# Two feed-forward blocks with mixers: the second mixer's norms by row sums on all partitions, its substitution loop in three runs

## The chip, the core and the metric

One core of a Trainium2 chip runs the whole program in one launch. The metric is device time in microseconds of that core; smaller is better. All names of engines are those of the profile: PE multiplies matrices (PEld is its weight load), DVE is VectorE, ACT is ScalarE, POOL is GpSimd, SP issues most DMAs.

## The reference, cut to what matters

A sequence of 512 tokens of width 1024 goes through two blocks, each: half a SwiGLU feed-forward, a mixer, half a SwiGLU feed-forward, a norm. All is float32. The change lies in the mixer of the second block, in two norms of it:

```
def short_conv_mixer(b_gate, c_gate, h, conv_w, out_gain):       # width 512, 8 groups of 64
    y = b_gate * causal_depthwise_conv(c_gate * h, conv_w)
    return rmsnorm per group of 64 channels of y, times out_gain
def gated_deltanet_mixer(q, k, v, z, b, a, ...):                 # 4 heads of 128
    q, k, v = split(silu(causal_depthwise_conv(qkv)));  q, k = l2norm(q), l2norm(k)
    o = gated_delta_rule_chunked(q, k, v, g, beta)   # per chunk: solve (I + lower) x = rhs, then a scan
    return rmsnorm(o, norm_w) * silu(z)              # over the 128 channels of a head
h = h + concat(y_conv, y_gdn) @ w_mix_out
```

Each rmsnorm is y * (mean(y*y) + eps) ** -0.5 * gain. The triangular solve is done by substitution inside blocks of 16 rows, then by merging blocks in three levels.

## The kernel before, in words

Activations lie with channels on the 128 partitions and the 512 tokens along the row, so a norm over channels needs a sum across partitions. That sum is made on PE. Every projection is made in three products of 128x512 in the type fp32r (high times high, high times low, low times high parts); a product of two float32 operands is issued by PE as two products, so one statement in the code shows as two instructions in the trace. A transpose of float32 shows as one.

`mix2` (L640) is the second mixer. PE's order in it is written by hand: `main` (L1023) runs 28 projections of 24 products each (`gproj`, L799, products at L806), and after every product `tick` (L1029) lets at most one waiting step of another generator run. A step that returns a lag n is due n ticks later. So 672 ticks make the stage, and the table `LAG` (L34) places every other product between the projections' ones. The generators are `chain` (L817, one for each of the 4 heads, at most 3 alive), `decays` (L726), and `short_end` (L970, one for each of the 4 short convolutions). The other engines' order is not by hand: the framework's scheduler sets it in advance, earlier statements first where they are ready.

The steps of a head's chain that the texts below speak of: the head's decays (L776 to L786: a spread of columns, Exp on ACT, four DVE operations at L783) and k's transposes (L823); q times k (L835); the sums of k's squares (`tok_sums`, L842); k times k and `u_` (L851, L854); transposes of v (L859) and of `u_` (L886); the products that give `bx` (L892); the substitution loop on DVE (L897 to L902: 15 turns of a product and a sum); three merging levels (L912, L914, ACT copies at L919 and L920, L924); `wt` (L929, L931); the scan over 4 chunks, each a product into `pv` (L940, L942), a copy `vn` by ACT (L943), after r0 ticks the products L949 and L954 and the state's update on DVE (L951, L953), which the next chunk's L942 reads after r1 ticks.

The head's norm at L957 to L966: squares, after o0 ticks `tok_sums` (L695, one product of 128x128 by 128x1 for each of 4 token blocks, `tok`=1 tick apart, so that a projection's product lies between), then `rsqrt_cols` (L237: a reciprocal root by 11 small DVE operations after one for scale and eps), after o1 ticks `spread2` (L704: four transposes at L267 that bring the columns back to all partitions), and one DVE operation with the gain. `short_end` does the same with two groups of 64: the spread is then eight float32 products (L270).

`rms_rows` (L281) is the form that the kernel uses elsewhere, for the norms ahead of the projections: the squares are split in a high and a low part (one ACT, one DVE operation), two products with a 128x128 matrix of minus ones (`onesr`, L278) give the sums on all partitions at once, then Ln, Exp and Square on ACT (L287 to L289) and two DVE operations (L290, L291) make the reciprocal root with one Newton step. Products into PSUM in `mix2` use three banks of the tag "g".

Of the kernel before, what the change touches and what calls it, by code (L numbers as in the profile page):

```python
# [10 lines left out]
F32 = mybir.dt.float32  # L11
F32R = mybir.dt.float32r
I32 = mybir.dt.int32
AF = mybir.ActivationFunctionType
ALU = mybir.AluOpType

P = 128
T = 512
NT = T // P
# [4 lines left out]
EPS = 1e-6  # L24
# [6 lines left out]
LIVE = 3  # L31
NWARM = 9
SCRATCH = 1024
LAG = dict(d0=4, d1=30, d2=81, d3=7, d4=10, tok=1, c0=7, c1=3, c2=3, c3=2, c5=17, c6=26, c7=46, c8=11, c9=9, c10=11, r0=3, r1=4, o0=9, o1=27, s0=14, s1=22)  # L34
MIXORD = (4, 5, 6, 0, 1, 2, 3, 7)
WINDOWS = (2, 4, 8, 16)
MAGIC = float(0x5F3759DF)
# [87 lines left out]
class Kern:  # L125
# [4 lines left out]
    def nm(self, s):  # L130
        self.n += 1
        return f"{s}_{self.n}"
# [8 lines left out]
def tile_blocks(ctx: ExitStack, tc: tile.TileContext, ins, out, stop=None):  # L141
    nc = tc.nc
    K = Kern(ctx, tc)
    nm = K.nm
    SM = [("sm", 1)]

    const = K.pool(ctx, "const", far=True)
# [4 lines left out]
    tp = K.pool(ctx, "tmp", far=True)  # L152
# [7 lines left out]
    def vcol(name, i=0, n=1):  # L160
        o = VEC_COLS[name][0] + i
        return vec[:, o : o + n]
# [3 lines left out]
        return cst[:, o : o + w]  # L166

    h = [hp.tile([P, T], F32, name=f"h{k}") for k in range(KD)]
    idle = const.tile([P, P], F32, name="idle")
    nc.vector.memset(idle, 0.0)  # L170
    nc.vector.memset(ones1, 1.0)
    warm = const.tile([P, 1], F32, name="warm")
# [2 lines left out]
    ident = cst_("ident")  # L175
# [61 lines left out]
    def rsqrt_cols(src, n, scale, eps=EPS):  # L237

        v = rp.tile([P, n], F32, name=nm("rv"), tag="rv", bufs=4)
        nc.vector.tensor_scalar(v, src, scale, eps, ALU.mult, ALU.add)  # L240
        return newton(v, n)
# [12 lines left out]
            yf = b  # L254
        return b

    def spread(psp, cols, groups=1):

        ps = psp.tile([P, T], F32, name=nm("pb"), tag=SM[0][0], bufs=SM[0][1])
        spread_into(ps, cols, groups)  # L260
        return ps

    def spread_into(ps, cols, groups=1):
        m = P // groups
        for t in range(NT):
            if groups == 1:
                nc.tensor.transpose(ps[:, t * P : (t + 1) * P], cols[:, t, :].to_broadcast([P, P]), ident)  # L267
                continue
            for g in range(groups):
                nc.tensor.matmul(ps[g * m : (g + 1) * m, t * P : (t + 1) * P],  # L270
                                 cols[:, t, g : g + 1].to_broadcast([P, m]), ident, start=True, stop=True)

    def row_sums(psp, parts, of, tag=None):

        tag, bufs = tag or SM[0]
        ps = psp.tile([P, T], F32, name=nm("pr"), tag=tag, bufs=bufs)
        for j, part in enumerate(parts):
            nc.tensor.matmul(ps, of, part, start=(j == 0), stop=(j == 1))  # L278
        return ps

    def rms_rows(psp, src, sq, y, scale, eps):  # L281

        parts = [tp.tile([P, T], F32R, name=nm("t"), tag="t", bufs=5) for _ in range(2)]
        split_into(*parts, src)
        yield
        ps = row_sums(psp, parts, onesr)
        nc.scalar.activation(y, ps, AF.Ln, scale=-scale, bias=epsc[:, EPSS.index(eps) : EPSS.index(eps) + 1])  # L287
        nc.scalar.activation(y, y, AF.Exp, scale=-0.5)
        nc.scalar.activation(sq, y, AF.Square, scale=math.sqrt(0.5 * scale))  # L289
        nc.vector.scalar_tensor_tensor(sq, ps, -eps / scale, sq, ALU.add, ALU.mult)  # L290
        nc.vector.scalar_tensor_tensor(y, sq, 1.5, y, ALU.add, ALU.mult)  # L291
        return y

    def col1(cols):
        return cols.rearrange("p (t o) -> p t o", o=1)

    class Prep:

# [341 lines left out]
    def mix2(prep, nxt):  # L640
# [3 lines left out]
        with ExitStack() as c:  # L644
            yp = K.pool(c, nm("yc"))
            yc, os_ = [None] * 4, [None] * GH
            with ExitStack() as c2:
# [12 lines left out]
                def gk(name, i=0):  # L660
                    o, n = CONST_COLS[name]
                    o += i * P - NKEEP
                    return gcst[:, o : o + min(n, P)]

                bdr = cp.tile([P, P], F32R, name=nm("bdr"))
                nc.scalar.activation(bdr, gk("bd"), AF.Copy)
                groups = gk("groups")

                offd = [cp.tile(S, F32, name=nm("offd")) for _ in range(3)]
                for y in offd:  # L670
# [9 lines left out]
                def bank(shape=S):  # L680
                    return psp.tile(shape, F32, name=nm("pg"), tag="g", bufs=3)
# [10 lines left out]
                def tb(x):  # L692
                    return x.rearrange("p (t o) -> p t o", o=1).to_broadcast(S)

                def tok_sums(s, n, rhs):  # L695

                    ps = bank([P, NT, n])
                    for t in range(NT):
                        if t:
                            yield LAG["tok"]  # L700
                        nc.tensor.matmul(ps[:, t, :], s[:, t * P : (t + 1) * P], rhs, start=True, stop=True)  # L701
                    return ps

                def spread2(cols, groups=1):  # L704
                    ps = bank([P, T])
                    spread_into(ps, cols, groups)
                    return ps


# [107 lines left out]
                def chain(hd, q, k, v):  # L817
# [21 lines left out]
                    yield LAG["c1"]  # L839

                    irk, es = ct(4), ct(4)
                    pn = yield from tok_sums(sk, 1, ones1)  # L842
                    rk = rsqrt_cols(pn.rearrange("p t o -> p (t o)"), NT, 1.0)
                    nc.vector.reciprocal(irk, rk)
                    nc.vector.tensor_tensor(es, rk, rk, ALU.mult)
                    nc.vector.tensor_tensor(es, es, bh, ALU.mult)
# [48 lines left out]
                    zc = ep.tile([P, NT, SB], F32, name=nm("zc"), tag="zc", bufs=2)  # L895
                    nc.gpsimd.tensor_copy(zc, gk("d16").rearrange("p (o c) -> p o c", o=1).to_broadcast([P, NT, SB]))
                    for i in range(SB - 1):  # L897
                        sb = ep.tile([P, NT, SB], F32, name=nm("sb"), tag="sb", bufs=2)
                        n = SB - 1 - i
                        nc.vector.tensor_tensor(sb[:, :, :n], bx[:, :, i, i + 1 :],  # L900
                                                zc[:, :, i : i + 1].to_broadcast([P, NT, n]), ALU.mult)
                        nc.vector.tensor_tensor(zc[:, :, i + 1 :], zc[:, :, i + 1 :], sb[:, :, :n], ALU.add)  # L902
# [55 lines left out]
                    nc.scalar.activation(so, po, AF.Square)  # L958
                    nc.vector.tensor_tensor(so, so, o, ALU.add)
                    nc.scalar.activation(o, po, AF.Copy)  # L960
                    yield LAG["o0"]
                    pn = yield from tok_sums(so, 1, ones1)
                    ro = rsqrt_cols(pn.rearrange("p t o -> p (t o)"), NT, 1.0 / P, EPS * EPS * P)
                    yield LAG["o1"]
                    pb = spread2(col1(ro))
                    nc.vector.scalar_tensor_tensor(o, o, vcol("gdn_out_norm_2"), pb, ALU.mult, ALU.mult)  # L966
                    os_[hd] = o
                    gate(hd)

                def short_end(i, yy):  # L970
                    sq = stmp()
                    nc.scalar.activation(sq, yy, AF.Square)
                    yield LAG["s0"]
                    pn = yield from tok_sums(sq, 2, groups)
                    cols = rsqrt_cols(pn.rearrange("p t o -> p (t o)"), 2 * NT, 1.0 / 64)
                    yield LAG["s1"]
                    pb = spread2(cols.rearrange("p (t o) -> p t o", o=2), 2)
                    nc.vector.scalar_tensor_tensor(yy, yy, vcol("conv_out_norm_2", i), pb, ALU.mult, ALU.mult)
                    yc[i] = yy

                chains, waiting, decayed, zs = [], [], [], [None] * GH
# [215 lines left out]
```

## Time and profile before

| | |
|---|---|
| median of 3 runs | 2250.54 us (2250.0 to 2250.67) |
| the profiled execution's own time | 2248.94 us |
| its span, first to last instruction | 2247.2 us |
| PE, DVE, ACT busy | 99%, 50%, 36% of the span |
| mean granted TensorE clock | 0.996 |

The span is the part of the execution that the profile shows; 1.74 us lie around it. Busy time of PE is modelled with its pipeline, so consecutive products overlap in the records and the step from one start to the next is what a product costs. A wait is the idle time of an engine ahead of an instruction, with the instruction that released it.

### The profile page before, as it was taken

To read this page: it belongs to the slowest core of one execution; us is meant where nothing else is said; L and a number is where in the kernel's file an instruction comes from. 1 tells how busy PE (TensorE), PEld (TensorE's weight loads), DVE (VectorE), ACT (ScalarE), POOL (GpSimd) and SP (SyncE) were. 2 spreads that over 40 slices of the span, in tenths; PEclk is the share of its full clock that TensorE was granted. 3 is DMA by queue.
4 is the path that set the end of the run, shared out by engine and by line. 5 is a ranking of instruction groups with operands and counts; after the bars stand their busy time and mean duration, and the time that the engine had idled before them with its cause. 6 is when DMAs were issued, how large, how long until landed. Compare 5 with 4: busy or idle time off the path is not lost. (4 is left out here: it accounts for less than half of the span.)

```text
span 2247.2 us, 25607 instructions
## 1 busy us (share of the span) xinstructions
PE 2224.5 (99%) x10438; PEld 1855.7 (83%) x10438; DVE 1124.7 (50%) x1709; ACT 815.4 (36%) x1075; POOL 35.9 (2%) x54
## 2 busy tenths in 40 slices
PE   9999999999999999999999999999989999999998
PEld 7888888888888888888888888888778888888887
DVE  6444334666564355444334644433787665444332
ACT  6233223444432234233234323222565344233321
POOL 0000000000220000000000000000000000000000
PEclk9999999999999999999999999999999999999999
DMA  5333333222233333333332333233211123332332
GB/s 165 96 102 94 96 94 113 87 90 76 85 103 96 101 94 94 98 99 94 96 94 92 104 98 99 89 103 99 78 57 38 57 76 94 96 102 94 96 96 71
DMA packets 61478, 208.20 MB, mean 93 GB/s; under 512 B 6832, under 2 KB 9392, under 8 KB 61360
## 3 DMA queue, kind: packets, MB, share of 16 engines
q1 hardware_dynamic: 58832, 203.48, 29.3%
q10 hardware_dynamic: 2528, 3.08, 0.4%
q8 instruction: 81, 1.33, 0.2%
q14 instruction: 37, 0.30, 0.0%
HBM read 204.44 MB, written 2.10 MB: 92 GB/s over the span
## 5 line engine op out<-in xcount | busy, mean ns | idle before, releaser
L214 PE MATMUL ps<-hi,wh 128*128 128x512 f32 (+1 forms) x2774 | 1076.3, 388 | 1.2 <-ACT wh L198 1.1
L215 PE MATMUL ps<-lo,wh 128*128 128x512 f32 (+1 forms) x2774 | 1075.5, 388 | 0.3 <-DVE lo L202 0.3
L216 PE MATMUL ps<-hi,wl 128*128 128x512 f32 (+1 forms) x2774 | 1075.4, 388 | 0.0
L198 ACT ACTIVATE wh<-wr 128x1024 fp32r<-128x1024 f32 (+2 forms) x392 | 407.3, 1039 | 1132.7 <-PE ps L215 615.7
L199 DVE TENSOR_TENSOR wl<-wr,wh 128x1024 fp32r<-128x1024 f32 (+2 forms) x392 | 468.9, 1196 | 329.4 <-ACT wh L198 328.6
L214 PEld LDWEIGHTS ps<-hi,wh 128*128 128x128 f32 x2774 | 521.2, 188 | 109.1 <-ACT wh L198 2.2
L215 PEld LDWEIGHTS ps<-lo,wh 128*128 128x128 f32 x2774 | 521.2, 188 | 108.6 <-DVE lo L202 1.6
L216 PEld LDWEIGHTS ps<-hi,wl 128*128 128x128 f32 x2774 | 521.2, 188 | 107.4 <-DVE wl L199 1.2
L362 DVE TENSOR_TENSOR t<-ps,rb 128x512 f32<-128x512 f32 x88 | 60.7, 690 | 258.0 <-PE ps L216 258.0
L359 DVE TENSOR_TENSOR t<-ps,rb 128x512 f32<-128x512 f32 x88 | 60.8, 690 | 169.5 <-PE ps L216 169.4
L198 ACT ACTIVATE hi<-t 128x512 fp32r<-128x512 f32 x119 | 75.2, 632 | 113.3 <-DVE t L364 63.2
L806 PE MATMUL ps<-hi,wh 128*128 128x512 f32 x224 | 92.7, 414 | 0.3 <-DVE t L988 0.3
L806 PE MATMUL ps<-hi,wl 128*128 128x512 f32 x224 | 92.4, 412 | 0.0
L806 PE MATMUL ps<-lo,wh 128*128 128x512 f32 x224 | 91.7, 410 | 0.0
L199 DVE TENSOR_TENSOR lo<-t,hi 128x512 fp32r<-128x512 f32 x119 | 83.5, 702 | 6.2 <-ACT hi L198 5.8
L364 DVE TENSOR_TENSOR t<-t,t 128x512 f32<-128x512 f32 x88 | 60.8, 691 | 8.3
L360 ACT ACTIVATE t<-t 128x512 f32<-128x512 f32 x88 | 54.1, 615 | 4.1 <-DVE t L359 4.1
L373 DVE SCALAR_TENSOR_TENSOR h<-ps,h 128x512 f32<-128x512 f32 x31 | 21.4, 692 | 60.4 <-PE ps L216 60.4
L806 PEld LDWEIGHTS ps<-hi,wh 128*128 128x128 f32 x224 | 42.7, 191 | 7.1 <-DVE t L988 0.8
L806 PEld LDWEIGHTS ps<-hi,wl 128*128 128x128 f32 x224 | 42.6, 190 | 6.5 <-issue 0.2
L806 PEld LDWEIGHTS ps<-lo,wh 128*128 128x128 f32 x224 | 42.5, 190 | 6.5 <-issue 0.2
L526 PE MATMUL pv<-wh,hi 128*128 128x256 f32 x128 | 36.3, 284 | 0.0
(291 smaller groups left out, 1293.5 us busy)
## 6 DMA issues: line engine op xcount, KB each, us to landing
wr<-in_ffn_w_in SPq DMA_DIRECT2D x174, 512.0 KB, 3.5
wr<-in_ffn_w_out SPq DMA_DIRECT2D x64, 512.0 KB, 3.5
wr<-in_w_in SPq DMA_DIRECT2D x48, 512.0 KB, 3.5
wr<-in_w_mix_in SPq DMA_DIRECT2D x28, 512.0 KB, 3.5
wr<-in_ffn_w_out SPq DMA_DIRECT2D x32, 384.0 KB, 3.1
wr<-in_w_v SPq DMA_DIRECT2D x8, 512.0 KB, 3.7
wr<-in_w_ret_up SPq DMA_DIRECT2D x8, 512.0 KB, 3.4
wr<-in_w_pool_up SPq DMA_DIRECT2D x8, 512.0 KB, 3.5
```

Source lines behind the costliest of these rows:

```text
L198: nc.scalar.activation(hi, src, AF.Copy)
L199: nc.vector.tensor_tensor(lo, src, hi.bitcast(F32), ALU.subtract)
L214: nc.tensor.matmul(ps, lh, rh, start=start, stop=False)
L215: nc.tensor.matmul(ps, lh, rl, start=False, stop=False)
L216: nc.tensor.matmul(ps, ll, rh, start=False, stop=stop)
L359: nc.vector.tensor_tensor(g, pg, rb, ALU.mult)
L360: nc.scalar.activation(g, g, AF.Silu)
L362: nc.vector.tensor_tensor(u, pu, rb, ALU.mult)
L364: nc.vector.tensor_tensor(m, g, u, ALU.mult)
L373: nc.vector.scalar_tensor_tensor(h[d], ps, 0.5, h[d], ALU.mult, ALU.add)
L526: nc.tensor.matmul(pv, xh[:, sl], wh[:, k % 4, :], start=(k == 0), stop=False)
L806: nc.tensor.matmul(ps, a[:, k, :], b, start=(k == j == 0), stop=(k == KD - 1 and j == 2))
```

## The change

`tok_sums` and `spread2` lose their group forms, and `tok_sums`, now used for k's squares alone, issues its four products one after the other without ticks between. `rms_rows` takes the matrix as an argument. `short_end` and the head's end call it: the split is made in the step of the squares, and s0 or o0 ticks later come the two products and the rest. For the short convolutions the matrix is `onesg`, minus ones inside the two groups of 64. The results y lie in tiles that are free in this stage (`prep.acc` for the short convolutions, `nxt.acc` for the heads). The substitution loop returns a lag of 16 ticks ahead of its turns 4 and 9 and after its end, where one lag of 46 stood after the end. Some lags of the table change. The zeros for the first products (`idle`) move to a rotating tile.

```
-LAG = dict(d0=4, ..., tok=1, c0=7, c1=3, c2=3, c3=2, c5=17, c6=26, c7=46, c8=11, c9=9, c10=11, r0=3, r1=4, o0=9, o1=27, s0=14, s1=22)
+LAG = dict(d0=4, ..., c0=9, c1=3, c2=3, c3=2, c5=19, c6=28, c7=16, c8=12, c9=9, c10=11, r0=4, r1=6, o0=14, s0=16)
-    idle = const.tile([P, P], F32, name="idle")
+    idle = tp.tile([P, T], F32, name="idle", tag="s", bufs=3)[:, :P]
-    def rms_rows(psp, src, sq, y, scale, eps):
+    def rms_rows(psp, src, sq, y, scale, eps, of=None):
...
-        ps = row_sums(psp, parts, onesr)
+        ps = row_sums(psp, parts, onesr if of is None else of)
...
-                groups = gk("groups")
+                onesg = cp.tile([P, P], F32R, name=nm("onesg"))
+                for i in range(2):
+                    nc.scalar.activation(onesg[:, 64 * i : 64 * i + 64], gk("groups")[:, i : i + 1].to_broadcast([P, 64]), AF.Copy, scale=-1.0)
...
-                def tok_sums(s, n, rhs):
-                    ps = bank([P, NT, n])
+                def tok_sums(s, rhs):
+                    ps = bank([P, NT])
                     for t in range(NT):
-                        if t:
-                            yield LAG["tok"]
-                        nc.tensor.matmul(ps[:, t, :], s[:, t * P : (t + 1) * P], rhs, start=True, stop=True)
+                        nc.tensor.matmul(ps[:, t : t + 1], s[:, t * P : (t + 1) * P], rhs, start=True, stop=True)
...
                     for i in range(SB - 1):
+                        if i in (4, 9):
+                            yield LAG["c7"]
...
+                    y = nxt.acc
+                    g = Steps(rms_rows(psp, so, so, y, 1.0 / P, EPS * EPS * P))
+                    g.step()
                     yield LAG["o0"]
-                    pn = yield from tok_sums(so, 1, ones1)
-                    ro = rsqrt_cols(pn.rearrange("p t o -> p (t o)"), NT, 1.0 / P, EPS * EPS * P)
-                    yield LAG["o1"]
-                    pb = spread2(col1(ro))
-                    nc.vector.scalar_tensor_tensor(o, o, vcol("gdn_out_norm_2"), pb, ALU.mult, ALU.mult)
+                    g.step()
+                    nc.vector.scalar_tensor_tensor(o, o, vcol("gdn_out_norm_2"), y, ALU.mult, ALU.mult)
...
                 def short_end(i, yy):
                     sq = stmp()
                     nc.scalar.activation(sq, yy, AF.Square)
+                    y = prep.acc
+                    g = Steps(rms_rows(psp, sq, sq, y, 1.0 / 64, EPS, onesg))
+                    g.step()
                     yield LAG["s0"]
-                    pn = yield from tok_sums(sq, 2, groups)
-                    cols = rsqrt_cols(pn.rearrange("p t o -> p (t o)"), 2 * NT, 1.0 / 64)
-                    yield LAG["s1"]
-                    pb = spread2(cols.rearrange("p (t o) -> p t o", o=2), 2)
-                    nc.vector.scalar_tensor_tensor(yy, yy, vcol("conv_out_norm_2", i), pb, ALU.mult, ALU.mult)
+                    g.step()
+                    nc.vector.scalar_tensor_tensor(yy, yy, vcol("conv_out_norm_2", i), y, ALU.mult, ALU.mult)
```

## Rows read from the trace of the kernel before

**Rows 1.** The page's first part: busy time, share of the span and number of instructions of each engine.
```profile
PE 2224.5 (99%) x10438; PEld 1855.7 (83%) x10438; DVE 1124.7 (50%) x1709; ACT 815.4 (36%) x1075; POOL 35.9 (2%) x54
```
**Rows 2.** Busy time by stretch over the second mixer (from its first projection product to the last): stretch, length, then busy time and number of instructions of each engine, granted clock, DMA share, GB/s.
```profile
1571.70:1600.00 28.30, 27.74 (x122) 20.58 (x122) 17.06 (x31) 17.10 (x24) 0.00 (x0) 1.00 0.30 95
1600.00:1650.00 50.00, 47.38 (x259) 38.97 (x258) 44.55 (x140) 28.53 (x41) 0.00 (x0) 1.00 0.19 64
1650.00:1700.00 50.00, 46.06 (x284) 39.54 (x283) 40.00 (x111) 29.49 (x54) 0.47 (x2) 1.00 0.17 54
1700.00:1750.00 50.00, 46.37 (x277) 40.96 (x276) 37.07 (x116) 25.20 (x45) 0.00 (x0) 0.93 0.14 43
1750.00:1800.00 50.00, 49.96 (x316) 43.64 (x315) 33.56 (x95) 18.11 (x32) 0.00 (x0) 1.00 0.17 54
1800.00:1830.20 30.20, 30.20 (x180) 24.67 (x179) 20.25 (x55) 12.46 (x20) 0.00 (x0) 1.00 0.23 70
sum 258.50, PE 247.72 PEld 208.36 DVE 192.48 ACT 130.90 POOL 0.47; mean PE 41.29 PEld 34.73 DVE 32.08 ACT 21.82 POOL 0.08
```
**Rows 3.** The waits of PE in the same stretch: who waited for whom, us in total, times, longest us.
```profile
PE pv L942 <- DVE st L953: 3.6, 1, 3.6
PE pg L835 <- ACT qkv L991: 2.3, 1, 2.3
PE pg L886 <- DVE u L854: 1.7, 1, 1.7
PE pg L914 <- ACT wt L931: 1.1, 1, 1.1
PE pg L929 <- DVE dec L783: 0.9, 1, 0.9
```
**Rows 4.** Busy time by stretch around the longest of these waits; the column after POOL is the granted clock.
```profile
1728.00:1729.00 1.00, 0.00 (x0) 0.00 (x0) 0.97 (x3) 0.97 (x3) 0.00 (x0) 0.61 0.00 0
1729.00:1732.00 3.00, 2.98 (x13) 2.88 (x14) 0.00 (x0) 1.92 (x3) 0.00 (x0) 0.50 0.00 0
1732.00:1735.00 3.00, 3.00 (x12) 2.62 (x12) 1.96 (x3) 0.60 (x1) 0.00 (x0) 0.50 0.00 0
```
**Rows 5.** Timeline of PE where one short convolution's sums by token block stand: start us, us, engine, line, operation, count.
```profile
1615.03 0.28 PE L701 MATMUL pg<-gcst,s 128*128 128x2 f32 x2
1615.17 0.48 PE L806 MATMUL ps<-hi,wh 128*128 128x512 f32 x1
1615.49 0.28 PE L701 MATMUL pg<-gcst,s 128*128 128x2 f32 x2
1615.62 0.48 PE L806 MATMUL ps<-lo,wh 128*128 128x512 f32 x1
```
**Rows 6.** Timeline of PE where a head's spread by transposes stands.
```profile
1717.77 0.60 PE L267 MATMUL pg<-cst,rb 128*128 128x128 f32 x4
1718.13 0.48 PE L806 MATMUL ps<-lo,wh 128*128 128x512 f32 x1
1718.44 0.40 PE L806 MATMUL ps<-hi,wl 128*128 128x512 f32 x1
```
**Rows 7.** Timeline of PE where a short convolution's spread stands (after a wait for the small DVE operations).
```profile
1625.56 1.09 PE L270 MATMUL pg<-cst,rb 128*64 128x128 f32 x16 [0.35 <-DVE ra L251]
1626.58 0.50 PE L806 MATMUL ps<-hi,wl 128*128 128x512 f32 x1
1626.92 0.40 PE L806 MATMUL ps<-hi,wh 128*128 128x512 f32 x1
```
**Rows 8.** Timeline of PE where the stage's own leading norm makes its row sums by two products on all partitions.
```profile
1580.62 0.62 PE L278 MATMUL pr<-t,onesr 128*128 128x512 f32 x2
1581.07 0.40 PE L806 MATMUL ps<-hi,wh 128*128 128x512 f32 x1
1581.30 0.39 PE L806 MATMUL ps<-lo,wh 128*128 128x512 f32 x1
```
**Rows 9.** Table loads of ACT that stand at the lines of `rms_rows`, whole span: count, duration ns min/median/max, first and last start.
```profile
L287 ACT ACT_TABLE_LOAD  x11: 1283/1283/1283, 32.1 to 1878.6; - x11
...
L288 ACT ACT_TABLE_LOAD  x11: 1283/1283/1283, 34.1 to 1886.1; - x11
```
**Rows 10.** Timeline of ACT behind that leading norm's two products (a weight split left out).
```profile
1581.27 0.69 ACT L287 ACTIVATE rb<-pr,epsc 128x512 f32<-128x512 f32 x1 [3.85 <-PE pr L278]
...
1582.92 1.28 ACT L288 ACT_TABLE_LOAD   x1
1584.22 0.63 ACT L288 ACTIVATE rb<-rb 128x512 f32<-128x512 f32 x1
1584.88 0.63 ACT L289 ACTIVATE acc<-rb 128x512 f32<-128x512 f32 x1
```
**Rows 11.** Timeline of DVE ahead of the end of PE's longest wait.
```profile
1727.26 0.86 DVE L783 SCALAR_TENSOR_TENSOR dec<-pg,c,gcst 128x128 f32<-128x128 f32 x3
1728.03 0.68 DVE L826 TENSOR_TENSOR ke<-pg,c 128x512 f32<-128x512 f32 x1
1728.63 0.34 DVE L953 SCALAR_TENSOR_TENSOR st<-st,c,pst 128x128 f32<-128x128 f32 x1
```
**Rows 12.** Groups by line on DVE in the stage: the small operation of the reciprocal root at L252; count, busy us, mean ns, idle before.
```profile
L252 DVE SCALAR_TENSOR_TENSOR ra<-ra,rv 128x4 f32<-128x4 f32 (+1 forms) x36 | 5.7, 161 | 0.8
```
**Rows 13.** The scan's copy by ACT, whole span: duration ns min/median/max, first and last start.
```profile
L943 ACT ACTIVATE vn<-pv,c x16: 348/367/369, 1688.8 to 1812.0; 128x128 f32<-128x128 f32 x16
```

More of the change, by code (lines that the diff above doesn't have):

```diff
@@ L33 @@
 SCRATCH = 1024
-LAG = dict(d0=4, d1=30, d2=81, d3=7, d4=10, tok=1, c0=7, c1=3, c2=3, c3=2, c5=17, c6=26, c7=46, c8=11, c9=9, c10=11, r0=3, r1=4, o0=9, o1=27, s0=14, s1=22)
+LAG = dict(d0=4, d1=30, d2=81, d3=7, d4=10, c0=9, c1=3, c2=3, c3=2, c5=19, c6=28, c7=16, c8=12, c9=9, c10=11, r0=4, r1=6, o0=14, s0=16)
 MIXORD = (4, 5, 6, 0, 1, 2, 3, 7)
@@ L255, in newton @@
         return b
[L257 to L271, printed above, removed]
     def row_sums(psp, parts, of, tag=None):
@@ L292, in rms_rows @@
         return y
-    def col1(cols):
-        return cols.rearrange("p (t o) -> p t o", o=1)
     class Prep:
@@ L693, in tb, with spread2 @@
                     return x.rearrange("p (t o) -> p t o", o=1).to_broadcast(S)
-                def tok_sums(s, n, rhs):
-                    ps = bank([P, NT, n])
+                def tok_sums(s, rhs):
+                    ps = bank([P, NT])
                     for t in range(NT):
-                        if t:
-                            yield LAG["tok"]
-                        nc.tensor.matmul(ps[:, t, :], s[:, t * P : (t + 1) * P], rhs, start=True, stop=True)
+                        nc.tensor.matmul(ps[:, t : t + 1], s[:, t * P : (t + 1) * P], rhs, start=True, stop=True)
                     return ps
-                def spread2(cols, groups=1):
+                def spread2(cols):
                     ps = bank([P, T])
-                    spread_into(ps, cols, groups)
+                    for t in range(NT):
+                        nc.tensor.transpose(ps[:, t * P : (t + 1) * P], cols[:, t, :].to_broadcast([P, P]), ident)
                     return ps
@@ L841, in chain @@
                     irk, es = ct(4), ct(4)
-                    pn = yield from tok_sums(sk, 1, ones1)
-                    rk = rsqrt_cols(pn.rearrange("p t o -> p (t o)"), NT, 1.0)
+                    rk = rsqrt_cols(tok_sums(sk, ones1), NT, 1.0)
                     nc.vector.reciprocal(irk, rk)
```

## The prediction

> **What bounds the kernel.** The page's first part comes first: PE is busy for 99% of the span, so whatever leaves PE's queue can leave the time [rows 1]. Busy PE is modelled with its pipeline, so the next view is the stretches of the stage that is edited: 258.5 us long, PE idle for 10.8 us of them, DVE busy 192.5 us and ACT 130.9 us [rows 2]. Nearly all of PE's idle time lies between 1600 and 1750; from 1750 on PE never stops. The waits of PE in the stage are few and each happens once: 3.6 us for the scan's state, 2.3 us for a Silu, 1.7, 1.1 and 0.9 us for others [rows 3]. The longest has a tail: after it the granted clock is 0.50, the lower of the two levels (1.2 GHz), for about 7 us [rows 4]. So this stage is bound by the number and kind of products in PE's queue, plus about 10.8 us of waits, plus what half a clock cost: 0.39 x 1.0 + 0.50 x 6.0 = 3.4 us [rows 4].
>
> The last fact that is needed is what a small product costs between large ones. Large ones step by 0.23 us (1581.07 to 1581.30) [rows 8]. One pair of sums by token block steps by 0.14 us, and the large product behind it takes 0.32 us instead of 0.23: the next pair starts 0.46 us after the first, so the pair costs 0.46 - 0.23 = 0.23 us [rows 5]. A change of kind on PE thus costs 0.09 us beside the product.
>
> **Products removed and added.**
> A head's norm loses four token-block pairs, each with a large product behind it: 4 x 0.23 = 0.92 us [rows 5]. It loses four transposes: 1717.77 to 1718.13 is 0.36 us, and 0.31 us for the large one behind, 0.08 over its step: 0.44 us [rows 6]. It gains two products on all partitions: 1580.62 to 1581.07 is 0.45 us, and the large one behind them takes its plain 0.23 [rows 8]. Net 0.92 + 0.44 - 0.45 = 0.91 us, four heads 3.6 us.
> A short convolution loses the same 0.92 us, and a spread of sixteen products: 1625.56 to 1626.58 is 1.02 us plus 0.34 - 0.23 = 0.11 us behind it, 1.13 us [rows 7]. It gains the same 0.45 us. Net 1.60 us, four of them 6.4 us.
> The sums of k's squares stay but stand in one block. Bounds: eight instructions at half of the pair's 0.14 us and one surcharge make 0.65 us, saving 0.27 us of 0.92; at the 0.09 us of a transpose [rows 6] they make 0.81, saving 0.11. I take the lower price, since it is the same instruction: 4 x 0.27 = 1.1 us (0.4 to 1.1).
> Sum of the products: **11.1 us less on PE** (10.4 to 11.1). Nothing hides it, as PE is the engine that never stops in the last 80 us [rows 2].
>
> **The other engines.** DVE: each norm gains the low part of the split and two row operations, 3 x 0.68 us by the nearest 128x512 operation [rows 11], and loses twelve small ones of 0.16 us [rows 12]: 16.3 us against at most 15.4 us in all. Even, so no term; the small ones overlapped in part, so up to 8 us more on an engine that is idle for 66 us of the stage [rows 2].
> ACT: each norm gains the high part (0.63), Ln (0.69), Exp (0.63), Square (0.63) and two table loads of 1.28 us: 5.1 us, 4.5 of it in one block behind the two products [rows 10]. Seven of the eight norms end late in the stage: counting `tick` through the new lags, the first short convolution's products stand at tick 161 of 672, the others at 395, 459, 497, 558, 569, 641 and 652. ACT is busy for 25.2 + 18.1 + 12.5 = 55.8 us of the 130 us from 1700 on [rows 2]; 7 x 5.1 = 36 us more make 92 of about 120. Not full, but dense.
> The two copies that make `onesg` go through ACT ahead of the stage's first norm. They are at most 0.37 us each by the 128x128 copy [rows 13]; the cover is ACT's own idle time there (17.1 busy of 28.3 us) [rows 2]. Without it 0.7 us; I take nothing.
> `idle` in a rotating tile: its products are the first of the program, nothing waits for that tile before the first norm's squares. Nothing.
> No DMA is added and none moved past; SP's queue and POOL's keep their order.
>
> **Waits that go and come.** The longest wait: DVE does the next head's decay and `ke` first and then the state's update L953, which ends when PE starts again [rows 11]. By the old lags the fourth head's decays stand at tick 410 and the third update at 412, read at 416. By the new ones the decays stay at 410 while the updates stand at 409, 419 and 429, read at 415, 425 and 435, since r1 goes from 4 to 6. So a different update sits next to the decay, and each has two large products more, about 0.5 us, to finish. The loop's second and third runs are later statements than before, so DVE prefers an update or a decay to them. I take the 3.6 us and the 3.4 us of half a clock as gone: 7.0 us (0 if another update is caught in the same way). The other waits of 1 to 2 us I leave: c0 gives the q-times-k step 0.5 us of its 2.3, c6 and c8 about as little.
> New waits: a `vn` (0.37 us, [rows 13]) or a merging copy may now queue behind Ln and Exp. The ticks show three such places: the second head's scan from 405 after the norm at 395, the third head's scan from 504 after 497, and the fourth head's last merging level at 566, between norms at 558 and 569, where also three banks serve five tiles. From below the price is nothing, from above the 4.5 us block each [rows 10]. In a static order ACT does whichever is ready first, so half of a block, less the 0.9 us that four ticks of r0 cover: about 1.3 us each, **4 us added** (0 to 13.5).
>
> Sum: 11.1 + 7.0 - 4 = 14 us less. Against the profiled execution's 2248.94 us that is 2234.9; the median of the runs is 1.6 us above that execution, so **2236.5 us**.
>
> **A rule against this.** ACT starts the Exp 0.02 us after its load's end, and every one of the 11 Ln and 11 Exp has its own load [rows 9, 10]. The Trainium skill, page "ScalarE: Activation LUTs", section "What ACT_TABLE_LOAD costs", puts a switch at about 2.66 us, 1.28 for the load and 1.38 for a drain, and under "Table sets: the hidden batching unit" it says that one set holds Ln and Exp, so that one load would do. The first part is not seen in these rows, and the second did not come about here. By the page's switch an estimate for ACT's late part is 7 x 2 x 1.38 = 19 us more, 111 of 120 us, and the slow case below would be the likelier; by the rows it is 92.
>
> **Rivals.**
> *Waits as large as now.* DVE already interleaves other work, so three runs may be nothing new, and another wait with its half clock takes the place of the old one. For it: the wait came from an update that was late by 3.6 us, and two ticks give 0.5. Against it: the new ticks part update and decay. Then 11.1 us alone count: 2239.4 us.
> *The waits go.* The new lags, longer at c0, c5, c6, c8, r0 and r1, clear nearly all: 11.1 + 10.8 + 3.4 = 25 us, 2225 us. Against it: the Silu wait of 2.3 us has table loads of its own, and there are now sixteen loads more.
> *ACT holds up PE, slower.* Place: Ln, Exp and their loads ahead of `vn`, `wt` and the merging copies in ACT's queue. Seven late norms, each 4.5 - 0.9 = 3.6 us, are 25 us against 18.1 gained: 2250.5 + 7 = 2257 us. It decides from 18.1 / 7 = 2.6 us a norm, more where a wait drops the clock as the longest one did [rows 4]. For it: ACT at 92 of 120 us with blocks of 4.5 us. Against it: ACT's part in the last 80 us is 30.6 busy [rows 2], so the backlog of one block is gone before the next norm at four of the seven. Half-way, at 2 us a norm, it eats the gain: 2246 to 2255, no change.
>
> **How the numbers follow.** A measurement of this kernel tells 0.2%, 4.5 us, from no change. Forecast 0.52 (2230 to 2243); waits as now 0.20 (2239 to 2246); the waits go 0.12 (2222 to 2230); ACT half-way 0.09; ACT slower 0.07. Faster is the first three, 0.84; same 0.09; slower 0.07. The range 2226 to 2247 leaves out most of the last two and the lower half of the third, some 0.2.
>
> **What would show it.** Right: PE's sums by row step 0.45 us for two, L806 behind them steps 0.23, no PE wait above 2 us, clock 1.00 in all stretches of the stage, the stage some 244 us long instead of 258.5, two loads a norm in ACT. Wrong: PE waits for `vn` or for the merging copies of over 2 us, or the stage's length falls by less than 6 us, or half clock elsewhere in it.

## The result and the profile after

The changed kernel takes 2270.32 us (2268.74 to 2270.79), the kernel before 2250.00 us: ratio 1.0089 (95% interval 1.0078 to 1.0100), about 20 us slower. The profiled execution's span is 2268.5 us.

Lines are those of each run's own kernel: a projection's product is L789 in the changed kernel (L806 before), the row sums of `rms_rows` are L262 (L278), its Ln and Exp L271 and L272 (L287, L288).

The page's first part answers to [rows 1]: ACT is busy 43.1 us longer, DVE 4.1 us.
```profile
PE 2227.3 (98%) x10310; PEld 1856.6 (82%) x10310; DVE 1128.8 (50%) x1637; ACT 858.5 (38%) x1128; POOL 35.9 (2%) x54
```
The stretches of the second mixer answer to [rows 2]; the last one reaches behind the last projection. Columns as there.
```profile
1571.70:1600.00 28.30, 27.74 (x123) 20.60 (x122) 17.23 (x31) 17.14 (x24) 0.00 (x0) 1.00 0.28 94
1600.00:1650.00 50.00, 42.38 (x201) 33.86 (x200) 39.80 (x91) 33.92 (x47) 0.00 (x0) 0.93 0.20 63
1650.00:1700.00 50.00, 43.17 (x219) 37.21 (x220) 36.91 (x130) 22.61 (x36) 0.47 (x2) 0.84 0.14 43
1700.00:1750.00 50.00, 46.90 (x287) 41.25 (x286) 35.55 (x90) 31.48 (x53) 0.00 (x0) 0.96 0.12 34
1750.00:1800.00 50.00, 46.60 (x275) 39.67 (x274) 38.20 (x91) 31.57 (x55) 0.00 (x0) 1.00 0.19 62
1800.00:1843.50 43.50, 40.36 (x204) 33.69 (x202) 24.21 (x34) 29.66 (x41) 0.00 (x0) 0.96 0.17 49
1843.50:1856.00 12.50, 7.54 (x20) 5.23 (x20) 9.05 (x14) 9.98 (x14) 0.00 (x0) 0.73 0.19 55
```
PE is idle for 284.3 - 254.7 = 29.6 us, where it was 11.0 us from the first projection product to as far behind the last. What the lower granted clock takes is one minus the clock column, times the length of the stretch: 0.07 x 50 + 0.16 x 50 + 0.04 x 50 + 0.04 x 43.5 + 0.27 x 12.5 = 18.6 us, where it was 3.4 [rows 4]. The last projection product starts 13.9 us later (1843.3 for 1829.4), and 7.4 us more are lost behind it.

PE's waits answer to [rows 3]: the longest of before, L953, is gone. In its place stand waits for DVE in the first half (`u` is the head's `u_`, `zu` the loop's result, `dec` the decays), for the scan's copy `vn`, for a merging copy `offd`, and for `hi`, the first split of the output projection.
```profile
PE pg L896 <- DVE zu L888: 5.6, 1, 5.6
PE ps L214 <- ACT hi L198: 5.0, 1, 5.0
PE pst L933 <- ACT vn L927: 4.5, 3, 2.7
PE pg L818 <- DVE dec L766: 3.4, 1, 3.4
PE pg L868 <- DVE u L836: 3.0, 1, 3.0
PE pg L913 <- DVE zu L909: 2.3, 1, 2.3
PE pg L898 <- ACT offd L903: 1.4, 1, 1.4
```
ACT's timeline around the 2.7 us of the scan's copy (PE's last product starts at 1733.90, its next at 1737.02): between Ln and Exp a Silu was put, so one norm brings three loads, and `vn` stands behind all, though PE began the product that it copies at 1732.98.
```profile
1730.84 1.28 ACT L271 ACT_TABLE_LOAD   x1
1732.13 0.69 ACT L271 ACTIVATE acc<-pr,epsc 128x512 f32<-128x512 f32 x1
1732.84 1.28 ACT L975 ACT_TABLE_LOAD   x1
1734.14 0.63 ACT L975 ACTIVATE qkv<-t 128x512 f32<-128x512 f32 x1
1734.78 1.28 ACT L272 ACT_TABLE_LOAD   x1
1736.08 0.63 ACT L272 ACTIVATE acc<-acc 128x512 f32<-128x512 f32 x1
1736.61 0.35 ACT L927 ACTIVATE vn<-pv,c 128x128 f32<-128x128 f32 x1
```
The norms' products came out as priced. PE's timeline, in answer to [rows 5, 8]: two row sums step 0.56 us in the place shown, 0.57 in one other and 0.46 or 0.47 in the other six, for 0.45 forecast, and the large one behind them 0.23. But the eight of k's squares in one block take 0.81 us and the large one behind them 0.32.
```profile
1615.33 0.72 PE L262 MATMUL pr<-t,onesg 128*128 128x512 f32 x2
1615.89 0.39 PE L789 MATMUL ps<-hi,wl 128*128 128x512 f32 x1
1616.12 0.40 PE L789 MATMUL ps<-hi,wh 128*128 128x512 f32 x1
...
1618.34 0.95 PE L682 MATMUL pg<-ones,s 128*128 128x1 f32 x8
1619.15 0.48 PE L789 MATMUL ps<-hi,wl 128*128 128x512 f32 x1
1619.47 0.39 PE L789 MATMUL ps<-hi,wh 128*128 128x512 f32 x1
```

### The profile page after: what moved, and what is told of

The parts are those of the page before. It is cut to its first block, busy times and chain, and to the rows that moved or that the text cites. A ratio compares the mean times of both kernels' runs of the same rounds, so it can differ in the third digit from the quotient of the medians.

```text
span 2268.5 us, 25327 instructions
## 1 busy us (share of the span) xinstructions
PE 2227.3 (98%) x10310; PEld 1856.6 (82%) x10310; DVE 1128.8 (50%) x1637; ACT 858.5 (38%) x1128; POOL 35.9 (2%) x54
## 5 line engine op out<-in xcount | busy, mean ns | idle before, releaser
L789 PE MATMUL ps<-hi,wh 128*128 128x512 f32 x224 | 92.4, 413 | 0.3 <-DVE t L972 0.3
L789 PE MATMUL ps<-hi,wl 128*128 128x512 f32 x224 | 92.7, 414 | 0.0
L789 PE MATMUL ps<-lo,wh 128*128 128x512 f32 x224 | 92.6, 414 | 0.0
L789 PEld LDWEIGHTS ps<-hi,wh 128*128 128x128 f32 x224 | 43.7, 195 | 8.3 <-DVE t L972 0.8
L789 PEld LDWEIGHTS ps<-hi,wl 128*128 128x128 f32 x224 | 44.0, 197 | 7.3
L789 PEld LDWEIGHTS ps<-lo,wh 128*128 128x128 f32 x224 | 43.6, 195 | 7.3
```

The source lines that it names most:

```text
L789: nc.tensor.matmul(ps, a[:, k, :], b, start=(k == j == 0), stop=(k == KD - 1 and j == 2))
```

## The experiments

Two theories were set against each other. **ACT**: the Ln and Exp of the new norms, with their table loads, queue ahead of what PE wants next. **Order**: the new lags and the three runs put statements of different heads in another order. In the table, loads are ACT's table loads from the first projection product to 10 us behind the last, and idle is PE's idle time from the first product to 30 us behind the last. Half clock is what the granted clock of 0.50 took there, half the length of its stretches. The last three columns are of one profiled execution each.

| run | median us | ratio to before (95%) | loads | idle us | half clock us |
|---|---|---|---|---|---|
| before | 2250.0 to 2250.7 | 1 | 19 | 11.0 | 3.4 |
| changed kernel | 2270.32 | 1.0089 (1.0078, 1.0100) | 38 | 29.6 | 18.8 |
| norms_only | 2262.12 | 1.0052 (1.0035, 1.0069) | 36 | 26.5 | 10.2 |
| norms_only_no_tables | 2245.56 | 0.9979 (0.9970, 0.9989) | 19 | 13.9 | 5.1 |
| no_tables | 2252.09 | 1.0005 (0.9996, 1.0015) | 21 | 18.0 | 11.9 |
| no_tables_last | 2261.03 | 1.0052 (1.0037, 1.0067) | 33 | 25.8 | 11.9 |
| lags_and_runs | 2255.81 | 1.0026 (1.0015, 1.0037) | 15 | 16.9 | 8.5 |
| after_one_run | 2264.14 | 1.0063 (1.0048, 1.0078) | 38 | 25.7 | 11.9 |
| runs_only | 2250.39 | 1.0001 (0.9992, 1.0009) | 19 | 12.1 | 5.1 |
| bx_first | 2257.72 | 1.0032 (1.0020, 1.0044) | 36 | 23.0 | 3.4 |
| bx_first_one_run | 2251.51 | 1.0005 (0.9996, 1.0013) | 36 | 19.2 | 8.5 |
| scan_lags | 2253.09 | 1.0013 (1.0004, 1.0021) | 19 | 13.7 | 6.8 |
| contig | 2252.74 | 1.0011 (1.0002, 1.0020) | 19 | 12.7 | 6.8 |
| shorts_new | 2254.86 | 1.0020 (1.0011, 1.0030) | 27 | 18.6 | 8.5 |
| heads_new | 2258.66 | 1.0035 (1.0022, 1.0048) | 28 | 17.5 | 8.5 |
| sqrt_old_order | 2267.92 | 1.0080 (1.0066, 1.0094) | 24 | 29.7 | 15.4 |
| shorts_12_new | 2252.12 | 1.0009 (1.0000, 1.0018) | 23 | 13.8 | 8.5 |
| shorts_012_late | 2251.12 | 1.0003 (0.9994, 1.0012) | 24 | 15.5 | 5.1 |
| last_old | 2249.11 | 0.9993 (0.9984, 1.0002) | 31 | 16.0 | 3.4 |
| last_old_first_late | 2249.82 | 0.9996 (0.9988, 1.0005) | 30 | 15.5 | 5.1 |

**The norms alone**, and the same without loads.
```
norms_only: the changed kernel with
-LAG = dict(..., c0=9, c5=19, c6=28, c7=16, c8=12, r0=4, r1=6, o0=14, s0=16)
+LAG = dict(..., tok=1, c0=7, c5=17, c6=26, c7=46, c8=11, r0=3, r1=4, o0=14, s0=16)   # one run, tok ticks back
norms_only_no_tables: the same, in the eight norms
-nc.scalar.activation(y, ps, AF.Ln, ...);     nc.scalar.activation(y, y, AF.Exp, scale=-0.5)
+nc.scalar.activation(y, ps, AF.Square, ...); nc.scalar.activation(y, y, AF.Copy, scale=-0.5)
```


> The new norms alone: lags of before for the chain and the sums of k's squares with a large product between, substitution loop in one run; only o0=14 and s0=16 are new. Theory ACT (Ln, Exp and their table loads queue ahead of the chain's Exp, the scan's copies and the last splits): most of the loss stays, 2260 to 2272 us, waits of PE of 20 us or more in the mixer. Theory order (the new lags put statements of different heads in another order): the products saved show, 2236 to 2246 us.

> The new norms in the old order (old lags, one run, sums of k's squares spaced) with Square and Copy in place of Ln and Exp (values are then not the norm's). Theory ACT with the table loads as the cause: the products saved, 10 us, show in the time, 2238 to 2245 us, waits of PE and half clock together within 4 us of the kernel before. Theory order, or ACT's work without loads as the cause: 2248 us or more.

Both came out as theory ACT has it (the second 0.6 us above its range): the norms alone lose 11.5 us, and without the loads the same instructions, in the same places on PE and but for a few swaps in the same order on ACT, gain 4.7 us. So 16.6 us hang on seventeen loads. The second run also bears out the price of the norms' products: its 4.7 us, with 2.9 us more idle time than before and 1.7 more of half clock, make 9.3 of the 10.0 forecast. PE's waits tell where the loads cost: for `hi` 4.5 us, for `u` up to 3.2, for `offd` 2.4 and for `zt` (the merging levels' other copy) 1.6 with loads; without loads `hi`, `offd` and `zt` are not on the list.
```profile
PE pg L870 <- DVE u L838: 4.9, 2, 3.2
PE ps L214 <- ACT hi L198: 4.5, 1, 4.5
PE pst L933 <- ACT vn L927: 3.0, 4, 1.1
PE pg L870 <- ACT offd L903: 2.4, 1, 2.4
PE pg L820 <- ACT qkv L975: 2.2, 1, 2.2
PE po L938 <- ACT vn L927: 1.6, 1, 1.6
PE pg L908 <- ACT zt L904: 1.6, 1, 1.6
```
And norms_only_no_tables:
```profile
PE pg L870 <- DVE u L838: 3.3, 2, 1.7
PE pg L820 <- ACT qkv L975: 2.2, 1, 2.2
PE po L938 <- ACT vn L927: 1.6, 1, 1.6
PE pg L898 <- ACT wt L915: 1.1, 1, 1.1
PE pst L933 <- ACT vn L927: 1.0, 1, 1.0
```

**The changed kernel without loads**, in all eight norms by the same replacement, and in the last short convolution and head alone (`tables=i < 3`, `tables=hd < 3`).

> The changed kernel with Ln replaced by Square and Exp by Copy in the eight norms of the second mixer (the values are then not the norm's; shapes, products and waits are the same), so that these norms need no table load. Theory ACT with the loads as the cause: 20 us or more of table loads go and most of the loss with them, 2240 to 2252 us. Theory order: at most 6 us better than the changed kernel, 2264 to 2270 us.

> The changed kernel with Square and Copy in place of Ln and Exp in the last short convolution and the last head alone (values there are not the norm's). If the 7.5 us that the changed kernel loses behind the last projection come from those norms' loads ahead of the splits for the output projection: 2262 to 2265 us, the wait for hi of 5.0 us gone. If it comes from elsewhere: 2268 us or more.

Without loads 18.2 us come back (2252.09, at the upper end of theory ACT's range), but the saved products still do not show: the waits for `zu` and `dec` stay (7.2 and 4.6 us). With the last two norms alone 9.3 us come back, 1 us more than expected at best, and the wait for `hi` falls to 0.3 us. In the changed kernel ACT's timeline there shows the last head's Ln and Exp, two loads and a third for the last Silu, in among the splits; the first split of a head (`hi<-o`), with which the output projection's order begins, comes at 1847.98.
```profile
1843.63 1.28 ACT L271 ACT_TABLE_LOAD   x1
1844.93 0.69 ACT L271 ACTIVATE acc<-pr,epsc 128x512 f32<-128x512 f32 x1
1845.51 0.62 ACT L198 ACTIVATE hi<-yy 128x512 fp32r<-128x512 f32 x1
1846.15 1.28 ACT L272 ACT_TABLE_LOAD   x1
1847.44 0.63 ACT L272 ACTIVATE acc<-acc 128x512 f32<-128x512 f32 x1
1847.98 0.61 ACT L198 ACTIVATE hi<-o 128x512 fp32r<-128x512 f32 x1
```

**Order.** Old norms with the new lags and runs; the changed kernel with one run; the kernel before with three runs; the changed kernel with `bx` three ticks earlier; both repairs; the scan's lags, with a shorter o1.
```
lags_and_runs: before, c0=9, c5=19, c6=28, c7=16, c8=12, r0=4, r1=6, and   +if i in (4, 9): yield LAG["c7"]
after_one_run: changed, without that yield, c7=48        runs_only: before, with that yield, c7=15
bx_first: changed, -c6=28 +c6=25     bx_first_one_run: both    scan_lags: before, r0=4, r1=6, o1=16
```


> The old norms with the new lags of the chain and the loop in three runs. Theory ACT: within 4 us of the kernel before, 2246 to 2254 us. Theory order: slower than before by what the waits of the changed kernel at dec, u and zu cost, 2258 to 2272 us, with waits of 3 us or more for DVE in the first half of the mixer.

Slower by 5.2 us, between the two ranges. Its projections take 258.4 us, as before 257.7: a wait for `zu` of 5.8 us came, and those of [rows 3] for the state, the Silu and `u_` went. 7.7 us are lost behind the projections, where the longer chain carries the old norm's o1=27 past the last one and PE waits 5.4 us for the small DVE operations. So with the old norms the new order costs next to nothing among the projections.

> The changed kernel with the substitution loop in one run again (one lag of 48 after it). If the three runs are the cause of the wait for zu (5.6 us and the clock behind it): 2260 to 2264 us. If not: 2268 to 2273 us.

> The kernel before with the substitution loop in three runs alone (three lags of 15 for one of 46). If a later statement for the second and third run lets DVE do the scan's update first, as forecast: the wait for st of 3.6 us and the half clock behind it go, 2243 to 2247 us. If the runs only make the loop end later: 2251 to 2257 us, with a wait for zu that the kernel before does not have.

The three runs cost 6.2 us in the changed kernel (2264.14, at the edge of the first range) and nothing in the kernel before, where neither expectation held; the wait for the scan's state, 3.8 us there, did not go.

> The changed kernel with c6=25 for 28: the first head's bx then stands at tick 216, ahead of the second head's decays at 217, as in the kernel before, and not at 219 behind them. Theory order: the waits for dec of 3.4 us and for zu of 5.6 us and the half clock between them shrink, 2256 to 2264 us. Theory ACT alone: 2267 to 2272 us.

12.6 us come back with three ticks (the profiled execution was its fastest, 2253.0 us). Counting `tick`, the old lags put `bx` of the first head at 216 and the second head's decays at 217; the new ones put `bx` at 219, behind them. ACT's timeline shows what came of it: in the changed kernel the copies L876 come last, behind five loads, at 1648.53, though PE has begun their last product at 1640.44. The five are those of the chain's Exp and of Silu; none is a new norm's, and no_tables has these copies late too, at 1646.76.
```profile
1638.28 1.28 ACT L761 ACT_TABLE_LOAD   x1
...
1639.77 1.28 ACT L975 ACT_TABLE_LOAD   x1
...
1642.33 1.28 ACT L763 ACT_TABLE_LOAD   x1
...
1644.76 1.28 ACT L975 ACT_TABLE_LOAD   x1
...
1646.70 1.28 ACT L769 ACT_TABLE_LOAD   x1
...
1648.53 1.06 ACT L876 ACTIVATE bx<-pg 128x512 f32<-128x512 f32 x2
```
With `bx` first they come at once, ten us earlier, and the whole stage has two loads fewer.
```profile
1638.85 1.06 ACT L876 ACTIVATE bx<-pg 128x512 f32<-128x512 f32 x2
```
So the loop starts at 1640.5 and not at 1651.3 (1638.3 before), the wait for `zu` is 3.0 for 5.6 us and the one for `dec` of 3.4 is gone.

But the swap of ticks is not enough by itself. lags_and_runs keeps the ticks between k's sums, so its `bx` stands at 222, further behind the decays at 217; yet its copies (L894 there) run at 1638.07 and 1639.49, ahead of the Exp of `dec` and the Silu behind it, and its loop starts at 1640.8.
```profile
1638.07 0.60 ACT L894 ACTIVATE bx<-pg 128x512 f32<-128x512 f32 x1
1639.49 0.60 ACT L894 ACTIVATE bx<-pg 128x512 f32<-128x512 f32 x1 [0.82 <-PE pg L893]
1639.98 0.62 ACT L786 ACTIVATE dec<-dec 128x512 f32<-128x512 f32 x1
```
What costs is the queue that the scheduler makes for ACT; why it puts `bx` last in the one kernel and not in the other is not shown.

> The changed kernel with both repairs of order: c6=25 (bx ahead of the second head's decays) and the loop in one run with one lag of 48. If the two repairs add (12.6 and 6.2 us): 2250 to 2254 us. If the three runs cost only where the loop starts late, as bx_first already mends: 2255 to 2260 us.

The repairs add: 18.8 us of the 20 are back, with 36 loads still there. Yet norms_only, which also has `bx` first and one run, with 36 loads and the same norms, is 10.6 us slower than this run; what differs are lags (c0, c5, c6, c8, r0, r1) and k's sums in one block. PE's idle time falls by 7.3 us and half clock by 1.7 between the two, so with the loads in place longer lags are worth something; which of them is not tested.

> The kernel before with r0=4 and r1=6 as in the changed kernel, and o1=16 for 27 so that the last head's norm does not move past the last projection. The step of the forecast that the longer scan lags end the wait for st of 3.6 us and the half clock of 3.4 us behind it: 2243 to 2246 us. If another update is caught in the same way, or the longer scan only moves the wait: 2249 to 2254 us.

The wait for the state shrinks to 1.9 us, yet the kernel is slower: a wait for the split `hi` of 2.5 us and other half clock take its place. The second expectation held. As o1 moved too, and `hi` stands at the stage's end, the loss is not the scan lags' alone.

**k's sums in one block**: `tok_sums` of the kernel before without its ticks, in all twelve places.

> The kernel before with the four products of every sum by token block in one block (no large product between). By the step of one pair, 0.14 us against 0.23, twelve sums save 0.27 us each: 2247 to 2248 us if the waits stay; by the step of a transpose, 0.09 us for each of eight instructions, 0.11 us each: 2249 us. The chains also come some ticks earlier, so a moved wait may add or take some 3 us.

2.5 us slower: the block saves nothing (0.90 us for 0.92 by the rows above), and waits moved.

**Which norms.** New norms in the short convolutions alone, in the heads alone; in the second and third short convolution; in the first three with the first one's sums 40 ticks behind its split; and Sqrt with a reciprocal for Ln and Exp.
```
shorts_new / heads_new: before, with only short_end's / only the head's end of the change
shorts_12_new: `if i in (1, 2)` new, else old      shorts_012_late: `if i < 3`, `yield 40 if i == 0 else 16`
sqrt_old_order: norms_only with
-AF.Ln ...; -AF.Exp ...   +nc.scalar.activation(y, ps, AF.Sqrt, ...); nc.vector.reciprocal(y, y)
```


> The kernel before with the new norms in the four short convolutions alone. PE saves 6.4 us by the priced products; ACT gains eight table loads. Theory ACT: the loss of both kinds together (11.5 us over before) is shared with the heads; the short norms end where the chain waits for ACT twice (first one beside the first head's decays, last one ahead of the output projection's splits), so 2250 to 2257 us. If only the heads' norms stand in the way: 2243 to 2246 us.

> The kernel before with the new norms in the four heads alone. PE saves 3.6 us; ACT gains nine table loads. Theory ACT: 2250 to 2257 us, with waits for the scan's copies and for the last splits. If only the short convolutions' norms stand in the way: 2245 to 2248 us.

Both kinds cost: 4.8 us, within the range of theory ACT, and 8.6, above it. Neither was free.

> The kernel before with the new norm in the second and third short convolution alone, whose blocks of Ln and Exp stand where the first head's decays and the last splits are not. Theory place (a block costs only where a step that PE wants within some ticks queues behind it): the products saved show, 2 x 1.6 us, 2246 to 2248 us. Theory loads (each norm costs by its loads wherever it stands; all four cost 4.8 us net): 2251 to 2254 us.

> The same with the first short convolution's norm new as well, its row sums 40 ticks after the split and not 16, so that its Ln stands behind the first head's Exp in the order. Theory place: one more product saving, 2244 to 2247 us, the wait for u back from 4.9 us to 1.7. Theory loads: 2252 to 2255 us.

The first, 2252.12 us, lies in the range of theory loads and not in that of theory place. Its trace leaves the two undecided: the only new waits are two for `vn`, 2.9 us together, so one of the two norms still met the scan; half clock of 8.5 for 3.4 us did the rest, most of it behind a wait of 2.2 us for a Silu that the kernel before has too, with 2.3 us [rows 3] and no half clock behind it. The second moved the Ln behind the first head's Exp, and the wait for `u` fell from 4.9 to 0.7 us as theory place has it; but a new one of 2.7 us for the loop's `zc` came, and the time, 2251.12 us, lies in neither range. 3.7 us of shorts_new's loss are back, of which the old norm in the last short convolution has a part; no gain over before is told from noise.

> The new norms in the old order (as the run of the new norms alone), with Sqrt on ACT and a reciprocal on DVE in place of Ln and Exp ahead of the same Newton step. Five table loads more than the kernel before, where Ln and Exp bring seventeen. Theory ACT with the loads as the cause: most of the difference between the new norms alone (2262) and those without loads (2245.6) comes back, 2245 to 2252 us, if the reciprocal takes about as long as another row operation of DVE (0.7 us); with a reciprocal of some us it would wait on DVE instead, 2255 us or more.

Slower than with Ln and Exp, though with twelve loads fewer: the reciprocal takes 3.34 us, 26.7 us of DVE in all, and waits for DVE (`zu` 5.5, `u` 4.5, `st` 4.1 us) come where those for `offd` and `zt` went, while the one for `hi` stays (4.4 us). So it does not test the loads alone.
```profile
L273 DVE RECIPROCAL acc<-acc 128x512 f32<-128x512 f32 x8 | 26.7, 3343 | 2.2 <-ACT acc L272 2.2
```

**Both causes mended**: bx_first_one_run with the old norm in the last short convolution and the last head (o0=9, o1=14, s0=14, s1=22 there), and that with the first short convolution's sums 40 ticks behind its split.

> The changed kernel with three repairs: c6=25, the loop in one run with c7=48, and the old norm for the last short convolution and the last head, so that no Ln stands ahead of the splits for the output projection. By the runs so far the two repairs of order give 2251.5, and the 7.2 us behind the last projection should go, less 2.4 us of products given back: 2245 to 2248 us, clear of both kernels. If the last norms' loads only move the wait: 2250 us or more.

> The same with the first short convolution's row sums 40 ticks after its split for 16, so that its Ln stands behind the first head's Exp. If that block is the cause of the wait for u of 3.0 us and the half clock behind it (6 us at half): 2240 to 2245 us. If not: as the kernel without it, 2245 to 2248 us.

2249.11 and 2249.82 us: 21 us better than the changed kernel, and not told from the kernel before. The 7.4 us behind the projections are gone, but waits of 16 us stand where 11 stood, so the forecast of a clear gain failed. In the second run the wait for `u` fell from 3.0 to 0.5 us and one of 2.9 us for `zc` took its place. The changed kernel with both its order mended and its loads taken out was not run.

## Why the prediction was wrong

**Products: right but for one term.** The norms' 10.0 us stand by the same rows to some 0.3 us. The sums of k's squares were priced at half of a pair (0.07 us) for each of eight; in a block they step 0.10 us, 0.90 us with the large one behind them, and saved 0.02 us a head, not 0.27. The cost lies above both bounds (0.65 and 0.81 us), so the term of 1.1 us was about 0.1.

**Sizes of the other engines: right.** ACT 43.1 us more (41 forecast), DVE 4.1 (0 to 8).

**The longest wait: it went, as forecast, but its 7.0 us do not show.** L953 is off the list in the changed kernel and in lags_and_runs. r0 and r1 alone do not do it: scan_lags left 1.9 us of it and did not gain.

**"The other waits of 1 to 2 us I leave": this step failed.** The forecast counted the ticks of the norms and of the scan and took the other lags only as slack. It did not count that c0, c5 and c6, less the three ticks that k's sums lose, carry `bx` from 216 past the second head's decays at 217, and did not ask what ACT's queue becomes then. There the copies of `bx` came last, behind five loads, with waits of 3.4 us for `dec` and 5.6 us for `zu` around it. bx_first prices that at 12.6 us, after_one_run the three runs behind it at 6.2.

**"4 us added" by ACT: this step failed in size and in place.** The loads cost 18.2 us in the changed kernel (no_tables) and 16.6 in the old order (norms_only against norms_only_no_tables). All three places that were named show, at more than the 1.3 us each: the second head's scan with 2.7 us for `vn`, the third's with 1.4, and the last merging level with 2.3 us, where DVE does a norm's row operations, which wait for ACT, ahead of `zu` (L909). Two more were not named: the first short norm, whose Ln and Exp with two loads (from 1615.10 on) stand ahead of the first head's Exp, so that DVE sits idle for it and `u` is late by 3.0 us,
```profile
1618.93 0.61 ACT L769 ACTIVATE dec<-dec 128x512 f32<-128x512 f32 x1
1619.58 0.69 DVE L820 TENSOR_TENSOR at<-pg,dec 128x512 f32<-128x512 f32 x1 [2.45 <-ACT dec L769]
```
and the splits for the output projection, 7.4 us. The price took half of a norm's block of 4.5 us, as if ACT did whichever is ready first; but its order is set in advance, so `vn` at 1736.61 stood behind the whole of it, and the Silu between Ln and Exp (load at 1732.84) made it longer still.

**Half clock was counted where a wait went and not where waits came**: 3.4 us became 18.8. New waits and half clock, 18.6 + 15.4, less 10.0 of products make 24.0. Of the idle time 5.1 us lie in stretches at half clock (0.8 before), so 2.1 are counted twice: 21.9, against spans that differ by 2268.5 - 2247.2 = 21.3. The rival "ACT holds up PE", at 0.07 and 2257 us, had half of the mechanism; it decided from 2.6 us a norm, and the loads alone cost 18.2 / 8 = 2.3, with the order on top. The two causes do not add up: 18.2 us come back by one and 18.8 by the other, 37 of the some 30 that were lost (20.3 and the 10.0 of products), so what a load costs here depends on the order around it.

The rule on tables bears on it: the Trainium skill, page "ScalarE: Activation LUTs", section "Table sets: the hidden batching unit", says to batch calls by set and that one set has Ln and Exp. The first agrees with norms_only_no_tables, which is 16.6 us faster without the switches; the second is not what this program got: in the whole span 19 loads stand at the Ln and 19 at the Exp line. The drain of 1.38 us that the same page of the Trainium skill, section "What ACT_TABLE_LOAD costs", adds to each load is not seen on either side of one (Ln to 1732.82, load from 1732.84, Silu at 1734.14).

What stays open: why the same wait is followed by half clock in one run and not in another, and so how much of each few-us difference between two orders is the order's own; and why the scheduler queued `bx` last.

## What to carry to other kernels

Where PE never stops, a product saved is worth its step only if the work that replaces it does not stand ahead, in the queue of an engine whose order is set in advance, of something that PE reads within the next few products; ask that for each place, the stage's end too. Price an activation in a mixed stream with its table load and with the load that the next one then needs. When lags in a hand-written order change, count the new order of every pair of steps that swaps, and look at the queues that the scheduler makes of it: one step three ticks earlier was worth 12.6 us here, while lags_and_runs had the same swap and hardly paid.

## What the runs showed of the hardware

Four pairs of 128x128 by 128x1 products take 0.81 us in one block, 0.10 us an instruction, close to the 0.09 us that a transpose over 128 columns takes [rows 6]; spaced between large ones a pair adds 0.23 us. A DVE reciprocal of 128x512 took 3.34 us where other 128x512 operations took 0.68. An activation table load took 1.28 us each time, and in the lines shown the next activation began 0.01 to 0.02 us behind it. During or just behind waits of PE of 1.2 to 5.6 us the granted clock fell to 0.50, the lower level of 1.2 GHz, for some 3 to 10 us: in seven stretches of the changed kernel and one of the kernel before. Other waits of 1.4 us in the changed kernel, and one of 2.3 us in the kernel before, had none.
